# 512 weight columns moving instead of 256 in the output projection and the FFN's second product

## Chip, cores and metric

One core of a Trainium2 chip runs the kernel. The metric is the device time of one execution in microseconds (us).

## What is computed

Two layers of a hybrid diffusion backbone over 512 latent tokens and 256 context tokens of width 1024, in fp32. Each layer has four token mixers and a SwiGLU FFN. What matters here is how each of the two sublayers ends:

```python
def merge_branches(outs, gate_cols, w_brs, w_out):
    gates = jnp.split(jax.nn.sigmoid(gate_cols), N_BRANCH, axis=-1)
    mixed = sum(g * (o @ w) for g, o, w in zip(gates, outs, w_brs))
    return mixed @ w_out

def swiglu(h, w1, w3, w2):
    return (jax.nn.silu(h @ w1) * (h @ w3)) @ w2
```

`w_out` is 1024 x 1024, `w2` is 2816 x 1024. After each sublayer x += gate * RMSNorm(result), and the next one's input is the modulated RMSNorm of x. The last layer needs the latent tokens alone.

## The kernel before

The tokens are cut into blocks of 128: six in layer 0 (four latent, two context), four in layer 1. Every fp32 product is made of three fp32r matmuls: both operands are split into a high and a low part (`split`, line 544: a copy to fp32r, then the rest by a subtraction on VectorE), and high x high, high x low and low x high are added in PSUM. `wload` (line 566) brings a weight slice of 256 columns in chunks of up to four row blocks through the buffers `raw`, `wh` and `wl`, three of each (`wpool`).

*The two products.* `project_out` (line 1938) multiplies the transposed activations by 256 columns of the weight at a time (`qq`, four of them). For each token block `tb`, `gemm_tm` (line 596) runs the whole depth into one bank of PSUM: the block's tokens are the stationary side, the 256 weight columns move. One instruction on 128 x 256 then copies the result to `y` or adds it to `y`. The output projection is one such pass over the first 512 rows of `w_out` and one `project_last` (line 1959) over the other 512. The FFN's second product is cut by depth into parts of 6, 6, 6 and 4 row blocks. Ahead of each part come the first-product steps `up` for it (tile `ps_u`); the first three parts go through `project_out`, the last through `project_last`. That one loads all its weights first (three quarters of them into tiles `wr` of the general pool `pU`), then goes block by block, and ScalarE squares each result for the norm (`ssq`).

*The border.* After each pair of blocks `border_pair` (line 700) follows: the sum of the squares, `rstd` (line 552, 12 small VectorE steps), scale and gate, the addition to the residual `xres`, the store, and `norm_x` for the next sublayer. `pre_pair` (line 659) then transposes `y` on TensorE and applies scale and shift (`hf`). `finish_out` (line 2015) sets the blocks of the next pair between the border of a pair and its transposes. In the last sublayer each block has its own border, which stores the output.

*Buffers.* PSUM has eight banks: four single ones (`tA`, pool `psA`) and two tiles of two banks (`tS`, pool `psS`), which the attention scores use. Tiles of up to 128 x 512 come from `pW`, which has 19 of them (`y`, `gcast`, `xres`, `hf` and others); tiles of up to 128 x 256 come from seven small ones (`t1`).

*The order.* The program is written in a logical order and recorded by `Plan` (line 46). A list scheduler then gives every engine its own order, from costs of its own for each instruction (`cost`, line 141) and from free buffers: an instruction whose tile finds no free buffer is passed over, and later ones may go first. Matmuls to the same place in PSUM are kept together in groups of up to 12. The engines keep the order thus written. All instructions are issued at line 406, so every row of the trace has this line, and one goes by tile names. `fill("out")` and `fill("ffn")` put modulation work (`ps_mod`) into the same stages. `run` runs steps one after the other, `weave` spreads one list over another.

Of the kernel before, what the change touches and what calls it, by code (L numbers as in the profile page):

```python
# [12 lines left out]
F32 = mybir.dt.float32  # L13
# [395 lines left out]
def trace(plan: Plan, a: dict, out: bass.AP, dbg=None, depth=2):  # L409
# [174 lines left out]

    def gemm_fm(ps, w, c0, xT, nk):

        for s0, s1, p in ps:
            n = 0
            for k in range(nk):
                wh, wl = w(k)  # L590
                for wt, xt in ((wh, xT[0][k]), (wh, xT[1][k]), (wl, xT[0][k])):
                    PE.matmul(p[:, :s1 - s0], lhsT=wt[:, c0:c0 + 128], rhs=xt[:, s0:s1],
                              start=(n == 0), stop=(n == 3 * nk - 1))
                    n += 1
# [64 lines left out]
    def pre_pair(l, kind, p, yq, hT):  # L659

        col = 0 if p < 2 else 1
        t0 = p * 256
        for f in range(0, 8, 2):
            ps = tA("ps_tr")
            fv = tW("hf", (128, 2, 256))
            for i in range(2):
                for j in range(2):
                    PE.transpose(ps[:, i * 256 + j * 128:i * 256 + (j + 1) * 128],
                                 yq[f // 2][:, j, i * 128:(i + 1) * 128], ident)
            for i in range(2):  # L670
                ft = f + i
                scaled(fv[:, i], ps[:, i * 256:(i + 1) * 256], modc[l, "sc_" + kind][:, ft, col:col + 1],
                       modc[l, "sh_" + kind][:, ft, col:col + 1])
                split(hT[0][ft][:, t0:t0 + 256], hT[1][ft][:, t0:t0 + 256], fv[:, i])

    def norm_x(xs, yq):
# [9 lines left out]
        for i in range(2):  # L686
            for q in range(4):
                scaled(yq[q][:, i], xs[i][q // 2][:, (q % 2) * 256:(q % 2 + 1) * 256], r[:, i:i + 1])
# [11 lines left out]
    def border_pair(l, kind, p, yq, ssq, gcast, x_src, x_dst, nxt, part=(0, 1)):  # L700
# [6 lines left out]
        for i in part:  # L707
            for q in range(4):
                sl = slice((q % 2) * 256, (q % 2 + 1) * 256)
                V.scalar_tensor_tensor(yq[q][:, i], yq[q][:, i], r[:, i - part[0]:i - part[0] + 1], gcast[q // 2][:, sl], op0=ALU.mult, op1=ALU.mult)  # L710
                V.tensor_tensor(xs[i][q // 2][:, sl], xs[i][q // 2][:, sl], yq[q][:, i], op=ALU.add)
            for hf in range(2):
                SP.dma_start(x_dst(2 * p + i)[:, hf * 512:(hf + 1) * 512], xs[i][hf])
# [1105 lines left out]
    def first_pair(p):  # L1819
        cell = {}  # L1820

        def norm():
            xs = load_x(lambda tb: a["xin"][tb * 128:(tb + 1) * 128], p)
            cell["y"] = [tW("y", (128, 2, 256)) for _ in range(4)]
# [23 lines left out]
    for l in range(depth):  # L1848
# [89 lines left out]
        def project_out(w_src, xT, nk, first, y):  # L1938

            cell = {}  # L1940

            def one(qq, tb):
                def go():
                    if tb == 0:
                        cell["w"] = wload([w_src[:, qq * 256:(qq + 1) * 256]], nk)
                    ps = tA("ps_out")
                    gemm_tm(ps[:, :256], cell["w"], 256, xT, nk, tb)
                    if first and tb % 2 == 0:
                        y[tb // 2][qq] = tW("y", (128, 2, 256))
                    yq = y[tb // 2][qq][:, tb % 2]  # L1950
                    if first:
                        copy(yq, ps[:, :256])
                    else:
                        V.tensor_tensor(yq, yq, ps[:, :256], op=ALU.add)
                return go

            return [lambda qq=qq: run([one(qq, tb) for tb in tbs]) for qq in range(4)]

        def project_last(w_src, xT, y, ssq):
# [4 lines left out]
            def load(qq):  # L1964
                def go():
                    src = w_src[:, qq * 256:(qq + 1) * 256]
                    if qq == 3:
                        w[qq] = wload([src], 4)
                        return
                    raw = wpool.tile([128, 4, 256], F32, tag="raw", name="raw")  # L1970
                    SP.dma_start(raw, src.rearrange("(k p) c -> p k c", p=128))
                    parts = []
                    for i in range(2):
                        parts.append([tU("wr", (128, 2, 256), F32R) for _ in range(2)])
                        split(parts[i][0], parts[i][1], raw[:, 2 * i:2 * i + 2])
                    w[qq] = lambda k: (parts[k // 2][0][:, k % 2], parts[k // 2][1][:, k % 2])
                return go

            def one(tb):
                for qq in range(4):  # L1980
                    ps = tA("ps_out")
                    gemm_tm(ps[:, :256], w[qq], 256, xT, 4, tb)
                    yq = y[tb // 2][qq][:, tb % 2]
                    V.tensor_tensor(yq, yq, ps[:, :256], op=ALU.add)
                    S.activation(t1("junk"), yq, AF.Square, accum_out=ssq[tb // 2][:, tb % 2, qq:qq + 1])

            return [load(qq) for qq in range(4)], [lambda tb=tb: one(tb) for tb in tbs]

        def borders(kind, y, ssq, nxt, hT):
# [5 lines left out]
            def pair(p, part=(0, 1)):  # L1995
                def go():
# [6 lines left out]
                    border_pair(l, kind, p, y[p], ssq[p], gate[0],  # L2003
# [4 lines left out]
            def pre(p):  # L2008
                return lambda: pre_pair(nxt[0], nxt[1], p, y[p], hT)
# [17 lines left out]
        y = [[None] * 4 for _ in range(3)]  # L2027
        ssq = [sm.tile([128, 2, 4], F32, tag=f"ssq{p}", name="ssq") for p in range(3)]
# [6 lines left out]
        y = [[None] * 4 for _ in range(3)]  # L2035
        ssq = [sm.tile([128, 2, 4], F32, tag=f"ssq{p}", name="ssq") for p in range(3)]
# [143 lines left out]
```

## Time and profile before

| | us |
|---|---|
| time, median of 3 runs | 3187.0 (3186.23 to 3187.34) |
| the profiled execution | 3185.25 |
| its span | 3183.2 |
| TensorE busy in it | 3061.0 (96%) |
| weight loads busy | 2717.3 (85%) |
| VectorE busy | 2037.1 (64%) |
| ScalarE busy | 1303.6 (41%) |

The profile is one execution. PE is TensorE's matmuls, PEld its weight loads, which run beside them; DVE is VectorE, ACT ScalarE, SP the queue that issues the DMAs. An instruction is written as out<-in with its tiles' names. Matmuls are pipelined, so what one costs is the time from its start to the start of the next, and not its duration. The granted clock is a share of 2.4 GHz.

### The profile page before, as it was taken

What the parts mean: (1) busy time and instruction counts of PE and PEld (TensorE: products, weight loads), DVE (VectorE), ACT (ScalarE), POOL (GpSimd) and SP (SyncE); (2) the same over time, 40 slices, a digit from 0 to 9 for tenths busy, and PEclk for the clock granted to TensorE, in tenths of its full rate; (3) what the DMA queues carried; (4) which work ended last, traced back from release to release, by engine and by line L of the source; (5) the groups of instructions that cost most, each with busy time, mean ns of one, the idle gap of its engine ahead of it and who ended that gap; (6) DMA issues with size and microseconds to landing.
All of it is one profiled execution on the core that took longest, in us unless ns stands there. A gap on an engine that the chain in (4) does not pass through costs nothing.

```text
span 3183.2 us, 50019 instructions
## 1 busy us (share of the span) xinstructions
PE 3061.0 (96%) x19658; PEld 2717.3 (85%) x19658; DVE 2037.1 (64%) x4289; ACT 1303.6 (41%) x2633; POOL 10.2 (0%) x24
## 2 busy tenths in 40 slices
PE   7999999999999999999999999899999999999998
PEld 4888888898898779898998987788978879989997
DVE  8556769998677565622322379888968678653445
ACT  6432335455565343522111254335545565442222
POOL 0000000000000000000000000000000000000000
PEclk8999999899999999999999999999999999999999
DMA  8544422523223764423223245235345234243332
GB/s 291 160 134 131 142 84 78 173 62 121 70 87 111 247 196 123 120 70 103 62 71 105 88 133 189 78 110 157 86 136 157 89 95 153 74 123 100 93 93 80
DMA packets 297195, 380.02 MB, mean 119 GB/s; under 512 B 24813, under 2 KB 224830, under 8 KB 296960
## 3 DMA queue, kind: packets, MB, share of 16 engines
q1 hardware_dynamic: 294368, 369.75, 37.3%
q0 software_dynamic: 2592, 7.08, 0.8%
q8 instruction: 155, 2.54, 0.3%
q14 instruction: 80, 0.66, 0.1%
HBM read 318.94 MB, written 57.83 MB: 118 GB/s over the span
## 4 chain that ended last, share of the span: by engine, by line
PE 84%; DVE 10%; ACT 3%; issue 2%; DMA 1%; SPq 0%; DVEq 0%; ACTq 0%
PE ps_u L406 19%; PE ps_out L406 13%; PE ps_gate L406 12%; PE ps_proj L406 7%; PE ps_hyin L406 5%; PE ps_ssdin L406 4%; PE ps_mla L406 2%; PE ps_v L406 2%; PE ps_ms L406 2%; PE ps_qk L406 2%; PE ps_z L406 2%; PE ps_mod L406 1%; PE ps_pT L406 1%; PE ps_s L406 1%; PE ps_spec L406 1%
## 5 line engine op out<-in xcount | busy, mean ns | idle before, releaser
L406 DVE TENSOR_TENSOR wl<-raw,wh 128x1024 fp32r<-128x1024 f32 (+2 forms) x342 | 397.3, 1165 | 309.1 <-ACT wh L406 304.6
L406 PE MATMUL ps_u<-hf,wh 128*128 128x512 f32 (+1 forms) x2240 | 571.3, 345 | 6.8 <-DVE hf L406 2.6
L406 ACT CAST wh<-raw 128x1024 fp32r<-128x1024 f32 (+1 forms) x296 | 294.9, 997 | 425.9 <-PE ps_out L406 148.3
L406 PEld LDWEIGHTS ps_u<-hf,wh 128*128 128x128 f32 x2240 | 391.5, 190 | 58.2 <-DVE hf L406 3.1
L406 PE MATMUL ps_gate<-h,wh 128*128 128x512 f32 (+1 forms) x1568 | 417.8, 355 | 3.6 <-ACT wh L406 1.4
L406 PE MATMUL ps_u<-hf,wl 128*128 128x512 f32 (+1 forms) x1120 | 385.7, 344 | 0.0
L406 PEld LDWEIGHTS ps_gate<-h,wh 128*128 128x128 f32 x1568 | 274.3, 190 | 45.4 <-issue 2.0
L406 PE MATMUL ps_gate<-h,wl 128*128 128x512 f32 (+1 forms) x784 | 276.1, 352 | 0.4 <-DVE wl L406 0.4
L406 PEld LDWEIGHTS ps_u<-hf,wl 128*128 128x128 f32 x1120 | 213.1, 190 | 25.3
L406 PE MATMUL ps_out<-wh,gTh 128*128 128x256 f32 x760 | 217.1, 286 | 0.0
L406 PE MATMUL ps_out<-wl,gTh 128*128 128x256 f32 x760 | 215.1, 283 | 0.0
L406 PE MATMUL ps_out<-wh,gTl 128*128 128x256 f32 x760 | 215.0, 283 | 0.0
L406 PEld LDWEIGHTS ps_gate<-h,wl 128*128 128x128 f32 x784 | 149.0, 190 | 21.4 <-DVE wl L406 0.8
L406 PE MATMUL ps_hyin<-h,wh 128*128 128x512 f32 (+1 forms) x576 | 154.8, 357 | 2.0 <-DVE zb L406 1.7
L406 DVE TENSOR_TENSOR y<-y,ps_out 128x256 f32<-128x256 f32 x160 | 66.9, 420 | 140.2 <-PE ps_out L406 139.2
L406 PEld LDWEIGHTS ps_out<-wh,gTh 128*128 128x128 f32 x760 | 145.9, 192 | 6.8 <-issue 4.9
L406 PEld LDWEIGHTS ps_out<-wl,gTh 128*128 128x128 f32 x760 | 145.9, 192 | 0.1
L406 PEld LDWEIGHTS ps_out<-wh,gTl 128*128 128x128 f32 x760 | 145.8, 192 | 0.0
L406 DVE TENSOR_TENSOR s1t<-s1t,ps_u 128x512 f32<-128x512 f32 (+1 forms) x70 | 40.1, 572 | 140.8 <-PE ps_u L406 140.8
L406 PE MATMUL ps_ssdin<-h,wh 128*128 128x512 f32 (+1 forms) x480 | 120.8, 343 | 1.6 <-DVE acrow L406 1.0
L406 ACT ACTIVATE gate<-ps_gate 128x512 f32<-128x512 f32 (+1 forms) x98 | 50.8, 518 | 165.1 <-PE ps_gate L406 145.7
L406 PEld LDWEIGHTS ps_hyin<-h,wh 128*128 128x128 f32 x576 | 101.7, 190 | 17.9 <-issue 3.0
(462 smaller groups left out, 7067.5 us busy)
## 6 DMA issues: line engine op xcount, KB each, us to landing
raw<-in_w_in SPq DMA_DIRECT2D x120, 512.0 KB, 4.1
raw<-in_ffn_w SPq DMA_DIRECT2D x120, 512.0 KB, 3.9
w_mod<-in_mod_w SPq DMA_DIRECT2D x96, 512.0 KB, 4.6
raw<-in_w_in SPq DMA_DIRECT2D x52, 256.0 KB, 3.2
d_gt<-gate SPq DMA_DIRECT2D x32, 384.0 KB, 2.5
gate_in<-d_gt SPq DMA_DIRECT2D x32, 384.0 KB, 4.3
d_spec<-spec SPq DMA_DIRECT2D x40, 256.0 KB, 3.9
gsp<-d_spec SPq DMA_DIRECT2D x40, 256.0 KB, 3.7
```

The source lines that it names most:

```text
L406: getattr(engines[e], method)(*map(place, args), **{k: place(v) for k, v in kw.items()})
```

## The change

Both products now move 512 weight columns per matmul. `project_out` goes by halves `hf` of 512 columns. In a half, all token blocks hold an accumulator of one bank each at once: the first four lie side by side in the two double tiles `tS`, the two context blocks of layer 0 in single banks. The weights come by `wload2` in chunks of two row blocks by 512 columns, and each chunk is used for all blocks, six matmuls each, before the next. After the last chunk each accumulator is copied or added to `y`, 128 x 512 at a time. `project_last` still goes block by block with single banks, by halves. `y` is now a tile of 128 x 512 for each block and half (before: 128 x 2 x 256 for each pair and quarter), and the border's instructions are 512 wide. The squares' throw-away output `junk` moves from the small pool to `pW`. Pool sizes, the filled-in work and the scheduler stay as they are. This is the core of the diff; the removed bodies stand in the kernel above, and most of their lines are left out here:

```diff
+    def wload2(src):
+
+        parts = [wpool.tile([128, 2, 512], F32R, tag=t, name=t) for t in ("wh", "wl")]
+        raw = wpool.tile([128, 2, 512], F32, tag="raw", name="raw")
+        SP.dma_start(raw, src.rearrange("(k p) c -> p k c", p=128))
+        split(*parts, raw)
+        return parts
...
             for i in range(2):
                 for j in range(2):
                     PE.transpose(ps[:, i * 256 + j * 128:i * 256 + (j + 1) * 128],
-                                 yq[f // 2][:, j, i * 128:(i + 1) * 128], ident)
+                                 yq[j][f // 4][:, (f % 4 + i) * 128:(f % 4 + i + 1) * 128], ident)
...
-            for q in range(4):
-                scaled(yq[q][:, i], xs[i][q // 2][:, (q % 2) * 256:(q % 2 + 1) * 256], r[:, i:i + 1])
+            for hf in range(2):
+                scaled(yq[i][hf], xs[i][hf], r[:, i:i + 1])
...
-            for q in range(4):
-                sl = slice((q % 2) * 256, (q % 2 + 1) * 256)
-                V.scalar_tensor_tensor(yq[q][:, i], yq[q][:, i], r[:, i - part[0]:i - part[0] + 1], gcast[q // 2][:, sl], op0=ALU.mult, op1=ALU.mult)
-                V.tensor_tensor(xs[i][q // 2][:, sl], xs[i][q // 2][:, sl], yq[q][:, i], op=ALU.add)
             for hf in range(2):
+                V.scalar_tensor_tensor(yq[i][hf], yq[i][hf], r[:, i - part[0]:i - part[0] + 1], gcast[hf], op0=ALU.mult, op1=ALU.mult)
+                V.tensor_tensor(xs[i][hf], xs[i][hf], yq[i][hf], op=ALU.add)
...
         def project_out(w_src, xT, nk, first, y):
-            cell = {}
-            def one(qq, tb):
+            def half(hf):
                 def go():
-                    if tb == 0:
-                        cell["w"] = wload([w_src[:, qq * 256:(qq + 1) * 256]], nk)
+                    ps = []
+                    for tb in tbs[:4:2]:
+                        s = tS("ps_out")
+                        ps += [s[:, 0:512], s[:, 512:1024]]
+                    ps += [tA("ps_out") for _ in tbs[4:]]
+                    for k0 in range(0, nk, 2):
+                        w = wload2(w_src[k0 * 128:(k0 + 2) * 128, hf * 512:(hf + 1) * 512])
+                        for tb in tbs:
+                            sl = slice(tb * 128, (tb + 1) * 128)
+                            n = 0
+                            for k in range(2):
+                                for xp, wp in ((0, 0), (0, 1), (1, 0)):
+                                    PE.matmul(ps[tb], lhsT=xT[xp][k0 + k][:, sl], rhs=w[wp][:, k],
+                                              start=(k0 == 0 and n == 0), stop=(k0 == nk - 2 and n == 5))
+                                    n += 1
+                    for tb in tbs:
+                        if first:
+                            y[tb][hf] = tW("y")
+                            copy(y[tb][hf], ps[tb])
+                        else:
+                            V.tensor_tensor(y[tb][hf], y[tb][hf], ps[tb], op=ALU.add)
+                return go
+            return [half(hf) for hf in range(2)]
+        def project_last(w_src, xT, y, ssq):
+            w = {}
+            def load(hf, kp):
+                def go():
+                    src = w_src[kp * 256:(kp + 1) * 256, hf * 512:(hf + 1) * 512]
+                    if (hf, kp) == (1, 1):
+                        w[hf, kp] = [[p[:, k] for k in range(2)] for p in wload2(src)]
+                        return
+                    raw = wpool.tile([128, 2, 512], F32, tag="raw", name="raw")
+                    SP.dma_start(raw, src.rearrange("(k p) c -> p k c", p=128))
+                    w[hf, kp] = [[tU("wr", (128, 512), F32R) for _ in range(2)] for _ in range(2)]
+                    for k in range(2):
+                        split(w[hf, kp][0][k], w[hf, kp][1][k], raw[:, k])
+                return go
+            def one(tb):
+                sl = slice(tb * 128, (tb + 1) * 128)
+                for hf in range(2):
                     ps = tA("ps_out")
-                    gemm_tm(ps[:, :256], cell["w"], 256, xT, nk, tb)
...
+                    n = 0
+                    for k in range(4):
+                        for xp, wp in ((0, 0), (0, 1), (1, 0)):
+                            PE.matmul(ps, lhsT=xT[xp][k][:, sl], rhs=w[hf, k // 2][wp][k % 2], start=(n == 0), stop=(n == 11))
+                            n += 1
+                    yq = y[tb][hf]
+                    V.tensor_tensor(yq, yq, ps, op=ALU.add)
+                    S.activation(tW("junk"), yq, AF.Square, accum_out=ssq[tb // 2][:, tb % 2, hf:hf + 1])
+            return [load(hf, kp) for hf in range(2) for kp in range(2)], [lambda tb=tb: one(tb) for tb in tbs]
...
-        y = [[None] * 4 for _ in range(3)]
-        ssq = [sm.tile([128, 2, 4], F32, tag=f"ssq{p}", name="ssq") for p in range(3)]
+        y = [[None] * 2 for _ in tbs]
+        ssq = [sm.tile([128, 2, 2], F32, tag=f"ssq{p}", name="ssq") for p in range(3)]
```

## Rows read from the trace of the kernel before

**Rows 1.** The page: busy time by engine; the chain that ended last.

```profile
PE 3061.0 (96%) x19658; PEld 2717.3 (85%) x19658; DVE 2037.1 (64%) x4289; ACT 1303.6 (41%) x2633; POOL 10.2 (0%) x24
...
PE ps_u L406 19%; PE ps_out L406 13%; PE ps_gate L406 12%; PE ps_proj L406 7%; PE ps_hyin L406 5%; PE ps_ssdin L406 4%; PE ps_mla L406 2%; PE ps_v L406 2%; PE ps_ms L406 2%; PE ps_qk L406 2%; PE ps_z L406 2%; PE ps_mod L406 1%; PE ps_pT L406 1%; PE ps_s L406 1%; PE ps_spec L406 1%
```

**Rows 2.** Stretches by stage: length, busy time of engines (instructions), clock, DMA.

```profile
1277.70:1314.00 36.30, 30.02 (x233) 28.57 (x231) 31.00 (x115) 28.36 (x75) 0.00 (x0) 0.95 0.58 176
...
1560.50:1612.30 51.80, 51.80 (x434) 51.80 (x433) 18.26 (x34) 6.50 (x8) 0.00 (x0) 1.00 0.23 72
...
1837.20:1886.00 48.80, 40.94 (x309) 39.71 (x309) 35.01 (x122) 25.45 (x82) 0.00 (x0) 0.93 0.34 109
...
2787.70:2810.00 22.30, 14.78 (x96) 13.61 (x95) 19.77 (x77) 15.64 (x38) 0.00 (x0) 0.85 0.64 203
...
2969.00:3003.60 34.60, 34.60 (x289) 34.56 (x289) 14.65 (x25) 6.55 (x8) 0.00 (x0) 1.00 0.35 107
...
3171.10:3183.20 12.10, 0.22 (x2) 0.01 (x1) 8.26 (x34) 0.51 (x2) 0.00 (x0) 0.72 0.28 108
```

**Rows 3.** The same view, `ps_out` alone: both layers, two product stages.

```profile
1200.00:1900.00 700.00, 271.29 (x2160) 264.22 (x2160) 41.66 (x100) 16.39 (x44) 0.99 0.31 96
2700.00:3183.20 483.20, 173.72 (x1440) 173.41 (x1440) 27.75 (x66) 11.15 (x30) 0.99 0.31 94
...
1560.45:1612.30 51.85, 51.77 (x432) 51.85 (x432) 9.68 (x23) 0.00 (x0) 1.00 0.23 72
2869.21:2903.75 34.54, 34.54 (x288) 34.49 (x287) 0.00 (x0) 5.58 (x15) 1.00 0.35 106
```

**Rows 4.** The same view, `ps_u` alone: the FFN's first product.

```profile
2903.75:2969.05 65.30, 65.30 (x288) 53.89 (x288) 3.44 (x5) 3.59 (x6) 1.00 0.30 89
...
1612.30:1712.45 100.15, 100.08 (x576) 88.59 (x576) 6.22 (x11) 5.89 (x12) 1.00 0.21 61
```

**Rows 5.** The same view, `ps_proj` alone: a merge.

```profile
2719.65:2741.55 21.90, 21.88 (x96) 17.94 (x96) 4.80 (x7) 1.00 0.26 79
```

**Rows 6.** Timeline of PE at its start: start us, us, instruction.

```profile
2719.67 0.50 PE L406 MATMUL ps_proj<-oT_mh,wh 128*128 128x512 f32 x1 [0.92 <-DVE oT_ml L406]
2720.01 0.40 PE L406 MATMUL ps_proj<-oT_ml,wh 128*128 128x512 f32 x1
2720.25 0.40 PE L406 MATMUL ps_proj<-oT_mh,wl 128*128 128x512 f32 x1
```

**Rows 7.** Groups by shape, 1200 to 1900 us: busy us, mean ns, idle before.

```profile
L406 DVE TENSOR_TENSOR wl<-raw,wh 128x1024 fp32r<-128x1024 f32 x64 | 78.1, 1224 | 145.3 <-ACT wh L406 144.8
L406 ACT CAST wh<-raw 128x1024 fp32r<-128x1024 f32 x59 | 61.8, 1047 | 108.3 <-PE ps_u L406 58.1 <-PE ps_out L406 25.4 <-DMA raw<-in_ffn_w 19.9
L406 DVE TENSOR_TENSOR y<-y,ps_out 128x256 f32<-128x256 f32 x96 | 40.0, 420 | 84.8 <-PE ps_out L406 84.1
L406 DVE SCALAR_TENSOR_TENSOR y<-y,rs_y,gcast 128x256 f32<-128x256 f32 x46 | 20.2, 481 | 0.1
L406 ACT ACTIVATE junk<-y 128x256 f32<-128x256 f32 x48 | 19.8, 413 | 29.9 <-DVE rs_w L406 10.6 <-DVE y L406 10.5 <-DVE rs_y L406 5.8
...
L406 DVE TENSOR_TENSOR s1t<-s1t,ps_u 128x512 f32<-128x512 f32 x20 | 13.8, 688 | 63.0 <-PE ps_u L406 63.0
L406 ACT ACTIVATE junk<-xres 128x512 f32<-128x512 f32 x22 | 13.3, 603 | 10.6 <-DVE xres L406 8.1 <-ACT junk L406 2.3 <-ACT wh L406 0.2
```

**Rows 8.** DMA issues: count, KB each, median us to landing.

```profile
raw<-in_ffn_w SPq DMA_DIRECT2D x120, 512.0 KB, 3.9
...
xres<-in_xin SPq DMA_DIRECT2D x24, 256.0 KB, 3.6
```

**Rows 9.** PE's waits in two border stretches: us, times, longest.

```profile
PE ps_out L406 <- ACT hf L406: 3.4, 1, 3.4
...
PE ps_out L406 <- DVE s1t L406: 1.1, 1, 1.1
...
PE ps_tr L406 <- ACT y L406: 3.9, 2, 3.5
```

## The prediction and its working

> **What bounds the kernel now.** I read the page first, then the stretches by stage, then the two tiles that differ only in the width of what moves, and last the waits at the borders. TensorE is busy 3061.0 us, 96% of the span, VectorE 64%, ScalarE 41%, and of the chain that ended last the matmuls on `ps_u` hold 19%, those on `ps_out` 13% [rows 1]. By stage: in the products the PE's share is full (51.80 of 51.80 us, 34.60 of 34.60) at a granted clock of 1.00, the upper of the two levels, 2.4 GHz [rows 2]. The PE idles where one sublayer hands over to the next, 6.3, 7.9 and 7.5 us in stretches of 36.3, 48.8 and 22.3 us, with the clock at 0.95, 0.93 and 0.85; and for the last 12 us, when the output is normalised [rows 2]. So in the stages that the change rewrites nothing but PE time counts: what VectorE, ScalarE or the DMAs gain or lose there is hidden until it stops the PE.
>
> **Part 1, the width.** The trace holds 2160 `ps_out` matmuls in layer 0 and 1440 in layer 1 [rows 3], 256 columns moving in each. A stage of nothing else gives their pace: 432 in 51.85 us and 288 in 34.54 us, both 120.0 ns each [rows 3]. What 512 columns cost is in the FFN's first product: 288 of 512 columns in 65.30 us, 226.7 ns in layer 1; in layer 0 100.15 us hold 288 of each width, and with 288 x 120.0 = 34.6 taken off, 65.6 / 288 = 227.7 ns [rows 4]. Two narrow ones (240.0) become one wide one, so 13.3 ns are saved per pair in layer 1 and 12.3 in layer 0. The reason can be seen too: beside the narrow ones the weight load is busy 34.49 of 34.54 us, beside the wide ones 53.89 of 65.30 [rows 3, 4], and the change halves the loads with the matmuls. The sum: 1080 x 12.3 = 13.3 us and 720 x 13.3 = 9.6 us, together 22.9 us, all on the path. The wide pace could be worse here, since the weights move and the tokens stand still; the merge, another 512-wide product, ran 96 in 21.90 us, 228.1 ns with its first wait in it [rows 5], and at that pace the gain is 1800 x 11.9 = 21.4 us. Those are my ends, 21.4 and 22.9; I take 22.9 because the FFN's 512-wide matmuls have the same input type and a full stage around them.
>
> The Trainium skill, "TensorE: Matmul & The Clock Gate", section "Back-to-back issue gap", gives the spacing of one matmul as its columns at 2.4 GHz plus about 2.5 ns. By that, one wide for two narrow would save 2.5 ns only, an estimate of 4.5 us for 1800. The rows measure 11 to 14 ns above the column time at both widths, so here the trace disagrees with it; it stands among the rivals.
>
> **Part 2, the order inside a product.** Before, each block of 128 tokens ran its whole depth in one bank; now 4 (layer 1) or 6 (layer 0) accumulators stay open, and the PE changes bank after 6 matmuls, 1.4 us. In the 432-matmul stage there are 24 chains, so 24 changes of bank, and its mean is still 120.0 [rows 3]: a change costs nothing that shows. Coming back to an open bank is in no row. I take 0; at the upper end, 220 changes (1320 wide matmuls by 6) could each cost one wait like the first matmul of the merge, which started 0.34 us before its successor in place of 0.23 [rows 6], so 0.11 x 220 = 24 us. A gain is excluded by the pace already being the steady one.
>
> **Part 3, drains and the banks they hold.** One drain adds 512 columns in 0.688 us where two took 0.420 each [rows 7]: 160 adds (96 in layer 0, two thirds as many in layer 1) become 80, 67 us of VectorE become 55, beside PE's work. A 2-bank tile comes free only when both its blocks are drained. Inside the last round of a half, block 0 is done while blocks 1 to 3 still run, so the drains overlap the matmuls: after block 1, the PE has blocks 2 and 3 left, 2 x 6 x 0.227 = 2.7 us in layer 1. A drain with one weight subtraction ahead of it in VectorE's order takes 1.224 + 0.688 = 1.9 us [rows 7]. So there is 0.8 us of cover; with two subtractions ahead, 3.1 us, it is short by 0.4. This can happen at the half-to-half change, 4 in layer 1; in layer 0 the cover is 5.4 us and two blocks use the single banks. I take 0, with 4 x 0.4 = 1.6 us as the near end. What waits behind a late drain is the first group of the second half, and on VectorE the next weight subtraction.
>
> **Part 4, weights.** A chunk is now two row blocks by 512 columns: 512 KB, landing in 3.9 us, cast in 1.05 and subtracted in 1.22 [rows 7, 8]; it feeds 4 x 6 x 0.227 = 5.4 us of PE in layer 1, 8.2 in layer 0. Only one chunk is in use at a time, where the six-deep product used two for all its blocks, so two of the three buffers are free to run ahead: 10.9 us of cover for 6.2 us of supply. Each FFN part takes 6 loads in place of 8; on SP's queue 24 loads of 256 KB and their casts go and 12 of 512 KB come. Nothing, as long as the run-ahead holds.
>
> **Part 5, the borders and the end.** Per pair of blocks 8 scale-and-gate and 8 adds of 256 columns (8 x 0.481 + 8 x 0.420 = 7.2 us, the adds priced as those to y) become 4 and 4; the 512-wide add is 0.688 and the gated form above it by the same 0.06, say 0.75: 5.8 us [rows 7]. Against that the last drain and square of a block are longer, 0.688 - 0.420 and 0.603 - 0.413, 0.5 us. So about 1 us less for each of eight pairs, while the PE's cover between borders shrinks from 96 x 0.120 = 11.5 to 48 x 0.227 = 10.9 us. Only the pair that the PE waits for counts. In two of the borders the longest waits were 3.4 and 3.5 us, for a normalised or a transposed tile [rows 9]. I take 1 us of gain for the whole; a bound above is all the idle time of the three borders, 21.7 us, of which half could go at best since the statistics chain itself keeps its 13 small steps; a bound below stands under the third rival. The last 12 us keep their length: two add-and-gate pairs are shorter by 0.4, the last drain longer by 0.5.
>
> **The sum.** The profiled execution took 3185.25 us, its span 3183.2, 2.05 us lying around it; the median of three is 3187.0, 1.75 above the profiled one. 3185.25 - 22.9 - 1 = 3161.4, plus 1.75 is 3163 us.
>
> **Rivals.**
> *The hand-over costs something.* The order of every engine is written ahead from the planner's own costs, so a drain or a cast can stand behind a later wait. At the eight half-to-half changes and the borders, 1.2 us each on about eight places takes 10 us back: 3173. For it: the sums of part 3 leave 0.8 us only. Against it: in the product stages of before the PE never stopped, with drains as dense and two weight buffers tied up [rows 2].
> *The borders open up.* Shorter chains and earlier starts (the first rounds need two depth blocks only, where the last product of layer 0 now waits 1.1 us for `s1t` [rows 9]) could take half of the 21.7 us: 3163 - 11 = 3152.
> *Slower: the 19 wide buffers run out.* The squares' junk moves from the small pool into the wide one. In layer 0's borders 12 y, 2 gate rows, 4 residual tiles and 1 transposed tile make 19 already. If a square must wait there until the next pair's residual tiles or y come free, the statistics come late, then the transposes. Priced by one residual load, 3.6 us [rows 8], in eight pairs, 29 us, plus 3 for the clock, which stood at 0.85 where the PE waited most [rows 2]: 3163 + 32 = 3195. It is slower than before from 24 us on, 3 us for every pair; at two thirds of the price it is 3184, no change. Against it: a junk tile lives for 0.6 us, and a y tile comes free soon after.
> *It does not do what it says: a wide matmul takes as long as two narrow ones.* The merge's second wide matmul started 0.24 us before the third, exactly 2 x 0.120 [rows 6]. At 238 to 240 ns throughout the gain is 0 to 3.6 us: 3184, no change. Against it: in the same merge the mean of 96 is 228.1, in the FFN 226.7. By the Trainium skill's spacing rule of part 1 the time would be 3182, an estimate and in effect this same case.
> *Bank cycling drops the clock.* If each change of bank left the PE idle briefly, as at the upper end of part 2, the granted clock could fall: the new products are 1800 x 0.227 = 409 us, and at 0.93, as in one border [rows 2], they take 31 us more: 3194. The Trainium skill, same page, section "A second HAM failure mode: psum-queue depth-cycling", tells of a 512-column kernel that cycled its banks and lost throughput so. Here the 24 changes at clock 1.00 speak against it [rows 2, 3].
>
> **Chances.** Forecast, 3156 to 3169: 0.62. Hand-over: 0.12. Borders open: 0.11. Wide buffers: 0.06 at the full price, 0.03 at two thirds of it. Wide as slow as two narrow: 0.04. Bank cycling: 0.02. The measurement can tell about 0.2%, 6.4 us. Faster by more than that: 0.62 + 0.12 + 0.11 = 0.85. Within it: 0.04 + 0.03 = 0.07. Slower: 0.06 + 0.02 = 0.08. The range takes in the first three cases with the paces' ends, 3151 to 3177.
>
> **What would show it.** `ps_out` 1800 times, a pure product stage of layer 1 in 144 x 0.227 = 32.7 us where it was 34.5, of layer 0 in 49.2 where it was 51.8, clock 1.00. Drains 80 of 0.69 us. The three border stretches within 2 us of before. Wrong would be: a start-to-start of 512-wide `ps_out` well above 228, idle time before `ps_out` put down to y or to `wh` inside a product, or ScalarE's squares waiting for a buffer. A stretch outside these stages that grows or shrinks by more than 3 us would be the planner's reordering, which no row here can price; a few us of it lie within the range.

## The result, and the profile after

| | before | after |
|---|---|---|
| time, median, us | 3187.17 (3186.23 to 3187.91, 4 runs) | 3154.08 (3153.45 to 3155.08, 4 runs) |
| profiled execution, its span, us | 3185.25, 3183.2 | 3153.45, 3151.4 |

The ratio is 0.9897, with a 95% interval of 0.9879 to 0.9914: faster by 33.1 us. The forecast was 3163, with a range of 3151 to 3177: the direction and the range held, and the gain was 9 us larger than forecast.

The page of after: the busy time of each engine; from its last part, the FFN's weight loads.

```profile
PE 3029.3 (96%) x17858; PEld 2614.4 (83%) x17858; DVE 2001.8 (64%) x4074; ACT 1295.2 (41%) x2500; POOL 10.1 (0%) x24
...
raw<-in_ffn_w SPq DMA_DIRECT2D x132, 512.0 KB, 3.8
```

Beside [rows 1] the PE has 1800 matmuls fewer and is busy for 31.7 us less, which is the whole gain of the span (31.8): its idle time over the whole span is the same, 122.2 and 122.1 us. Part 1's sum for the width is 22.9 us, so some 9 us of PE time went from matmuls that the change leaves alone; the mean granted clock of the profiled execution is 0.981 before and 0.983 after. VectorE was busy for 35 us less and ScalarE for 8, beside the PE; part 5 below comes to where VectorE's time counts.

The stretches of after with `ps_out` alone, to be read beside [rows 3]: window, length, busy time of PE, weight loads, DVE and ACT (instructions), clock, DMA share, GB/s. First each layer, then one pure product stage of each.

```profile
1200.00:1900.00 700.00, 251.50 (x1080) 201.01 (x1080) 32.74 (x49) 12.98 (x23) 0.99 0.33 101
...
1555.90:1604.90 49.00, 49.00 (x216) 40.37 (x216) 7.21 (x11) 0.00 (x0) 1.00 0.25 75
2844.50:2877.15 32.65, 32.60 (x144) 26.87 (x144) 0.00 (x0) 3.23 (x6) 1.00 0.37 110
```

216 in 49.00 us are 226.9 ns each, 144 in 32.65 are 226.7 ns, at clock 1.00 and with the PE busy throughout. The weight load no longer fills the stage (26.87 of 32.65).

The stages of after, beside [rows 2]; all five engines now have a column. In order: layer 0's mixer border, the hand-over to layer 1 in two pieces, layer 1's mixer border, the last 12 us.

```profile
1275.20:1311.40 36.20, 30.09 (x193) 27.31 (x191) 30.74 (x107) 27.79 (x65) 0.00 (x0) 0.91 0.58 196
1826.70:1865.80 39.10, 35.50 (x163) 28.69 (x161) 30.02 (x87) 20.15 (x53) 0.00 (x0) 1.00 0.37 119
1865.80:1965.10 99.30, 96.19 (x540) 81.63 (x541) 95.52 (x231) 56.74 (x108) 2.11 (x4) 0.98 0.68 213
2762.65:2785.20 22.55, 14.28 (x94) 13.01 (x94) 18.79 (x68) 15.98 (x36) 0.00 (x0) 0.85 0.51 172
3139.40:3151.40 12.00, 0.15 (x1) 0.00 (x0) 8.19 (x27) 0.72 (x2) 0.00 (x0) 0.72 0.26 101
```

Two borders and the end are as long as before (36.20, 22.55 and 12.00, where they were 36.30, 22.30 and 12.10). The hand-over is not: 39.10 us where [rows 2] has 48.80, at clock 1.00 where it had 0.93. And the piece behind it, layer 1's first input products, is shorter as well; the same view of before, and the two pieces taken as one, before and after:

```profile
1886.00:1989.60 103.60, 98.18 (x541) 83.17 (x540) 96.97 (x241) 55.73 (x105) 2.11 (x4) 0.97 0.61 196
```

```profile
1837.20:1989.60 152.40, 139.12 (x847) 122.88 (x847) 131.98 (x363) 81.18 (x187) 2.11 (x4) 0.96 0.52 168
```

```profile
1826.70:1965.10 138.40, 131.69 (x703) 110.32 (x702) 125.55 (x317) 76.89 (x160) 2.11 (x4) 0.99 0.59 187
```

The piece behind holds the same 540 matmuls but for two, none of them touched by the change: 99.30 against 103.60 us.

To put the whole gain in its places, both traces are cut at the starts of the same eight matmuls. All table entries here and below are differences between such starts, in us, each from one execution (of the 23 of before on one chip the fastest took 3181.3 us and the slowest 3193.1, so a microsecond or two in one stretch shows little); "width" is what part 1's sum gives for the stretch.

| stretch | before | after less before | width |
|---|---|---|---|
| start to the last merge matmul of layer 0 (not touched) | 1210.9 | +0.9 | 0 |
| to layer 0's last mixer-border transpose (output projection) | 102.4 | -3.4 | -3.5 |
| to layer 0's last `ps_u` (FFN, three products) | 523.8 | -8.0 | -8.0 |
| hand-over: to the middle of layer 1's `ps_hyin` | 152.4 | -14.0 | -1.8 |
| to the last merge matmul of layer 1 (not touched) | 751.8 | +2.0 | 0 |
| to layer 1's last mixer-border transpose | 68.3 | -2.2 | -2.6 |
| to layer 1's last `ps_u` | 337.1 | -5.8 | -5.7 |
| to the end | 36.4 | -1.3 | -1.3 |
| sum | 3183.2 | -31.8 | -22.9 |

Five stretches give what the width alone gives, within 0.4 us. All that goes beyond it, 12.2 us, lies in one place, the hand-over, and 2.9 are lost again in work that the change doesn't touch. The hand-over's PE was busy for 139.1 us of 152.4 before, and for 131.7 of 138.4 after: 7.4 less busy, of which 1.8 is width and 5.6 go with the higher clock (0.96 and 0.99), and 6.6 less idle.

### The profile page after: what moved, and what is told of

Same layout as the page of the kernel before. It is cut to its first block, busy times and chain, and to the rows that moved or that the text cites. A ratio compares the mean times of both kernels' runs of the same rounds, so it can differ in the third digit from the quotient of the medians.

```text
span 3151.4 us, 45961 instructions
## 1 busy us (share of the span) xinstructions
PE 3029.3 (96%) x17858; PEld 2614.4 (83%) x17858; DVE 2001.8 (64%) x4074; ACT 1295.2 (41%) x2500; POOL 10.1 (0%) x24
## 5 line engine op out<-in xcount | busy, mean ns | idle before, releaser
L406 ACT CAST wh<-raw 128x1024 fp32r<-128x1024 f32 (+3 forms) x297 | 306.6, 1033 | 454.4 <-PE ps_out L406 177.4
L406 PE MATMUL ps_out<-wh,gTh 128*128 128x512 f32 x380 | 149.2, 392 | 0.2
L406 PE MATMUL ps_out<-wl,gTh 128*128 128x512 f32 x380 | 148.1, 390 | 0.0
L406 PE MATMUL ps_out<-wh,gTl 128*128 128x512 f32 x380 | 148.1, 390 | 0.0
L406 PE MATMUL ps_qk<-h,wh 128*128 128x512 f32 (+1 forms) x448 | 114.7, 346 | 1.4 <-ACT rope_sw L406 0.9
L406 PE MATMUL ps_mla<-wh,h 128*128 128x256 f32 (+1 forms) x544 | 104.6, 285 | 1.7 <-DVE zb L406 1.3
L406 PE MATMUL ps_hyin<-h,wl 128*128 128x512 f32 (+1 forms) x288 | 102.3, 355 | 0.0
L406 ACT ACTIVATE s1t<-ps_u 128x512 f32<-128x512 f32 (+1 forms) x70 | 35.3, 504 | 152.0 <-PE ps_u L406 152.0
```

The source lines that it names most:

```text
L406: getattr(engines[e], method)(*map(place, args), **{k: place(v) for k, v in kw.items()})
```

## Experiments

Three theories stood on the 10 us beyond the width. A: they are VectorE's time at the borders, from instructions 512 wide. B: they are the scheduler's order, which any edit draws anew. C: they come from the layout of `y`, one tile for each block and half, which ties no block to its neighbour. First the two halves of the change were taken apart.

### The new order of work with narrow matmuls (narrow_new_order)

```diff
-                    for k0 in range(0, nk, 2):
-                        w = wload2(w_src[k0 * 128:(k0 + 2) * 128, hf * 512:(hf + 1) * 512])
+                    for k0 in range(0, nk, 4):
+                        m = min(4, nk - k0)
+                        w = wload([w_src[k0 * 128:(k0 + m) * 128, qq * 256:(qq + 1) * 256]], m)
...
-                                    PE.matmul(ps[tb], lhsT=xT[xp][k0 + k][:, sl], rhs=w[wp][:, k],
+                                    PE.matmul(ps[tb], lhsT=xT[xp][k0 + k][:, sl], rhs=w(k)[wp],
```

Accumulators side by side and held open as after, but 256 columns of each move; `project_last` does its halves as two chains of 256.

> The changed kernel with its new order but 256 columns moving again: in project_out the accumulators of all blocks stay open over chunks of four row blocks by 256 columns (drains 256 wide), project_last runs each half as two 256-wide chains; squares and border stay 512 wide. If the width is worth 22.9 us (1080 x 12.3 + 720 x 13.3 ns) and the order nothing: 3154 + 22.9 = 3177 us, product stages at 120.0 ns per matmul. If the order or the earlier start of the products made part of the gain, it stays well below, 3165 to 3170. If open accumulators cost something that the width hid, above 3185.

Measured: 3193.39 us, ratio 1.0019 (1.001 to 1.0029). Its pure product stage, `ps_out` alone, and a stretch far ahead of any changed work with the wait that it holds (us, times, longest):

```profile
2875.95:2910.50 34.55, 34.55 (x288) 34.50 (x287) 0.00 (x0) 4.53 (x14) 1.00 0.35 107
```

```profile
1120.00:1160.00 40.00, 29.47 (x216) 20.29 (x219) 14.33 (x33) 11.39 (x24) 0.00 (x0) 0.83 0.78 264
```

```profile
PE ps_mod L406 <- DMA w_mod<-in_mod_w: 8.6, 3, 7.8
```

In the product 288 take 34.55 us, 120.0 ns each as in [rows 3]: the order inside a product and the open banks give and cost nothing there. The two FFN stretches are 1.3 us shorter and 2.4 longer than before's, where after's are 8.0 and 5.8 shorter: nearly all of that is the width. The hand-over is 7.9 us shorter than before's although no matmul in it is wider; part 5 below comes back to this. The 16 us above the expected time are in other places: the stretch up to layer 0's last merge matmul, with the same instructions as before, grew by 15.3 us, part of it the PE's wait of 8.6 us for a modulation weight, with the clock at 0.83 around it. Nothing of the edit acts there but the scheduler. That was the first sign for B, and the time, 3193, is outside every forecast made for it but the last, "above 3185", whose cause it doesn't have.

### Borders and layout without the wide products (border_wide_only, border_narrow, layout_only)

border_wide_only is the kernel before with `y` as after and the border's instructions as after; matmuls, drains and squares keep 256 columns:

```diff
-                    yq = y[tb // 2][qq][:, tb % 2]
+                    yq = y[tb][qq // 2][:, qq % 2 * 256:qq % 2 * 256 + 256]
...
-            for q in range(4):
...
             for hf in range(2):
+                V.scalar_tensor_tensor(yq[i][hf], yq[i][hf], r[:, i - part[0]:i - part[0] + 1], gcast[hf], op0=ALU.mult, op1=ALU.mult)
+                V.tensor_tensor(xs[i][hf], xs[i][hf], yq[i][hf], op=ALU.add)
```

border_narrow is the kernel after with the border's three kinds of instructions cut to 256 columns:

```diff
+            for q in range(4):
+                hf, sl = q // 2, slice((q % 2) * 256, (q % 2 + 1) * 256)
+                V.scalar_tensor_tensor(yq[i][hf][:, sl], yq[i][hf][:, sl], r[:, i - part[0]:i - part[0] + 1], gcast[hf][:, sl], op0=ALU.mult, op1=ALU.mult)
+                V.tensor_tensor(xs[i][hf][:, sl], xs[i][hf][:, sl], yq[i][hf][:, sl], op=ALU.add)
```

layout_only is border_wide_only with that same cut: every instruction as before, only the tiles of `y` are the new ones.

> The kernel before with the border alone made 512 wide (scale, gate, add, normalise; y kept per block and half); matmuls, drains and squares stay 256 wide. Theory A: the gain beyond the width, about 9 us, is VectorE time at the hand-over to layer 1, where VectorE was busy 77 of 82 us, so it comes back here: 3177 to 3182 us, and the stretch from the last FFN product of layer 0 to the first Hyena input product shrinks by 6 us or more. Theory B: those 9 us are the scheduler's order falling another way: a shift of either sign up to 8 us at places that have nothing to do with the border, 3179 to 3195, and no tie to that stretch.

> The changed kernel with its border alone cut back to 256-wide instructions (scale, gate, add, normalise). Theory A: the time beyond the width's is lost again, 3159 to 3164 us, at the hand-over to layer 1. Theory B: a shift of either sign, 3147 to 3162, wherever the order falls differently.

> The kernel before with y kept in one 128 x 512 tile per block and half in place of one 128 x 2 x 256 tile per pair and quarter; every instruction as before, 256 wide. Theory C, the layout itself (which y tiles come free when) makes the extra gain at the hand-over to layer 1: about 3178 us, that stretch 8 us or more shorter. Theory B, any new order of the scheduler moves that stretch: either sign, 3178 to 3195, and no reason for the same 8 us. Theory A, VectorE instruction width: no gain, 3187.

Measured: border_wide_only 3177.79, ratio 0.9973 (0.9961 to 0.9984); layout_only 3175.8, ratio 0.9972 (0.9963 to 0.9982); border_narrow 3153.84, ratio 0.9896 (0.9881 to 0.9911), the time of after. So in a freshly drawn order the width of the border's instructions adds nothing on either side, and the layout alone has the 8 us of border_wide_only. Where they lie, as the difference to before (border_wide_only's profiled execution was 5 us faster than its median):

| stretch | after | layout_only | border_wide_only | border_narrow |
|---|---|---|---|---|
| first, not touched | +0.9 | -3.9 | -0.9 | -0.7 |
| layer 0's FFN | -8.0 | 0.0 | 0.0 | -8.0 |
| hand-over | -14.0 | -5.9 | -8.0 | -11.0 |
| layer 1's FFN | -5.8 | 0.0 | 0.0 | -5.8 |

The hand-over of layout_only, one stretch for the two of before (48.80 in [rows 2] and the 103.60 above), and what its PE waited for:

```profile
1832.00:1978.50 146.50, 133.50 (x847) 117.11 (x846) 130.80 (x367) 82.24 (x189) 2.11 (x4) 1.00 0.54 176
```

```profile
PE ps_out L406 <- DVE y L406: 3.6, 2, 2.6
...
PE ps_out L406 <- ACT hf L406: 1.7, 1, 1.7
```

146.50 us where it was 152.4, and the difference is PE busy time: 133.5 us for the same matmuls that took 139.1 (847 records in both), at a clock of 1.00 in place of 0.96. The idle time is the same, 13.0 and 13.3 us; but the one wait of 3.4 us for `hf` [rows 9] is now 1.7, and the longest is 2.6. So 5.6 of the 5.9 us are not a wait that went: the idle time comes in shorter pieces, and the clock stays at its upper level. That the one makes the other isn't shown. Around one and the same wait, 2.6 us of `ps_out` for `y`, the clock was 0.89 in before and 1.00 in layout_only:

```profile
1855.00:1870.00 15.00, 12.42 (x92) 12.22 (x91) 12.33 (x49) 7.63 (x26) 0.00 (x0) 0.89 0.23 79
```

```profile
1849.80:1864.80 15.00, 12.43 (x104) 12.01 (x102) 13.12 (x53) 8.59 (x29) 0.00 (x0) 1.00 0.31 112
```

It isn't the chance of one execution either: in all ten of layout_only the mean clock of the span is 0.984 to 0.986, in the 17 of before beside them 0.979 to 0.983. Here the clock goes with the order; what in the order does it stays open.

### The last product narrow (last_narrow)

The kernel after with `project_last` of before (256 columns, squares in four parts):

```diff
-                for hf in range(2):
+                for qq in range(4):
...
+                    gemm_tm(ps[:, :256], w[qq], 256, xT, 4, tb)
+                    yq = y[tb][qq // 2][:, qq % 2 * 256:qq % 2 * 256 + 256]
+                    V.tensor_tensor(yq, yq, ps[:, :256], op=ALU.add)
```

> The changed kernel with project_last as it was before, 256 columns and 256-wide drains and squares, project_out wide. 480 of the 1800 wide matmuls (288 in layer 0, 192 in layer 1) are two narrow ones again: 288 x 12.3 + 192 x 13.3 ns = 6.1 us back, 3160 us if only the width counts. Theory A adds the drains and squares at the hand-overs, 1 to 3 us: 3161 to 3163. Theory B: 3152 to 3168.

Measured: 3165.1, ratio 0.9933 (0.9919 to 0.9948): 11.0 us above after, where the width of these 480 pairs is 6.1. `project_out`, which stays wide, keeps its pace to the last digit, and the hand-over has waits of the PE for banks that after doesn't have (the border's `norm_x` writes `junk` to a bank of `tA`):

```profile
2855.15:2887.80 32.65, 32.62 (x144) 26.84 (x143) 0.00 (x0) 3.23 (x6) 1.00 0.37 109
```

```profile
PE ps_out L406 <- ACT junk L406: 4.7, 3, 1.7
```

Against after, the hand-over is 5.8 us longer, 4.0 more than its width, layer 0's border 2.4 (1.8 of it width) and the first stretch, which isn't touched, 1.6. The excess is again at the hand-over, and again mixed with a new order; theory A's 3161 to 3163 is missed, B's 3152 to 3168 holds.

### The border's width with the order held (border_split_same_order)

To price A without B, the kernel after keeps the order of the scheduler, and every instruction on 512 columns that writes `y` or `xres` (drains, which read `ps_out`, and DMAs excepted) is issued as two of 256 at its place:

```diff
+                        names = [self.tiles[v.name][3] for v in args if isinstance(v, bass.AP) and v.name in self.tiles]
+                        wide = names[0] in ("y", "xres") and "ps_out" not in names and method != "dma_start" and self.cols(args[0]) == 512
+                        for sl in (slice(0, 256), slice(256, 512)) if wide else (None,):
+                            cut = lambda v: v[:, sl] if sl and isinstance(v, bass.AP) and self.cols(v) == 512 else v
```

> The changed kernel with the scheduler's order of every engine held exactly; only at issue each 512-wide border instruction (scale, gate, add, normalise) becomes two of 256 in its place. Theory A: VectorE time bounds the hand-overs, some 0.8 us per pair on eight pairs, so 3154 + 4 to 8 = 3158 to 3162. Theory B: the width of these instructions is worth next to nothing, 3153 to 3156, and border_narrow's equal time was no accident of order.

Measured: 3163.14, ratio 0.9944 (0.9928 to 0.9961), 9.1 us above after by the medians; the two ran on different chips, and by the ratios, each to before on its own chip, it is 15 us. Groups of after, 1200 to 1900 us (out<-in, shapes, count | busy us, mean ns | idle before, releaser):

```profile
L406 DVE SCALAR_TENSOR_TENSOR y<-y,rs_y,gcast 128x512 f32<-128x512 f32 x24 | 17.2, 746 | 0.1
L406 DVE TENSOR_TENSOR xres<-xres,y 128x512 f32<-128x512 f32 x24 | 15.8, 683 | 0.0
```

The same groups of border_split_same_order, whose instructions are issued at line 410, and its hand-over:

```profile
L410 DVE SCALAR_TENSOR_TENSOR y<-y,rs_y,gcast 128x256 f32<-128x256 f32 x48 | 20.3, 479 | 0.1
...
L410 DVE TENSOR_TENSOR xres<-xres,y 128x256 f32<-128x256 f32 x48 | 17.5, 417 | 0.0
```

```profile
1830.00:1971.50 141.50, 133.36 (x703) 111.38 (x701) 128.59 (x347) 78.50 (x167) 2.11 (x4) 0.98 0.56 184
```

Two narrow gates cost 0.958 us for 0.746, two narrow adds 0.834 for 0.683. The hand-over is 3.1 us longer than after's 138.4, half of it PE busy time at a lower clock (133.36 against 131.69); the front stretch is 2.9 longer, layer 1's border 1.2, the end 0.8. So A is real as long as the order is held: the two intervals don't meet, and VectorE's time is worth 8 us between the two traces, 9 to 15 by the times. border_narrow, with the same widths and an order made for them, lost none of it. Either the scheduler buys back what the instructions cost or its order happened to be a good one; in both cases A can't be read off a kernel whose order is drawn again.

### Three orders for each kernel (before, after and layout_only with the latency at 118 and 138 ns)

The scheduler takes 128 ns for the latency behind an instruction of VectorE and 135 behind ScalarE's. These two numbers change no instruction, only the order:

```diff
-        LAT = {"V": 128.0, "S": 135.0,
+        LAT = {"V": 138.0, "S": 145.0,
```

and 118 and 125 in the runs named v118.

> The kernel before, the same instructions, with the scheduler's assumed latency behind VectorE and ScalarE 10 ns longer (138 and 145 in place of 128 and 135), so that its order falls a little differently. Theory B: the time moves by several us, and the stretch of the hand-over to layer 1 by as much as in the variants (5 to 14 us) in some of these orders: 3175 to 3200. Theories A and C: within 3 us of 3187, the hand-over stretch unchanged.

> The kernel before with the scheduler's assumed latency behind VectorE and ScalarE 10 ns shorter (118 and 125). As for the longer one: by theory B 3175 to 3200 with the hand-over stretch moving, by theories A and C within 3 us of 3187.

> The changed kernel with the scheduler's assumed latency behind VectorE and ScalarE 10 ns longer (138 and 145). The kernel before came out 6 to 9 us slower in each of its two other orders. If the change is worth 22.9 us by width plus some 8 by the border's wide instructions in any order, this one is about 31 us under the kernel before in the same order: near 3162, between 3156 and 3168. If a part of the 33 us was a lucky order, the gap to the same order of before shrinks to 24 or less: 3168 or above. In all of them the pure product stages stay at 227 ns per matmul.

> The changed kernel with the assumed latencies 10 ns shorter (118 and 125). As for the longer ones: 3156 to 3168 if the gain does not hang on the order, 3168 or above if a part of it did.

> Layout only (y per block and half, all instructions 256 wide as before) in the order of the 10 ns longer latencies. If the layout itself gains 8 us it is 8 us under the kernel before in this order, about 3185; if its gain was one draw of the order it is anywhere from 3180 to 3200.

> Layout only in the order of the 10 ns shorter latencies. If the layout itself gains 8 us, about 3184; if its gain was one draw of the order, anywhere from 3180 to 3200.

| latency | before | layout_only | after | after less before |
|---|---|---|---|---|
| 128, as given | 3187.2 | 3175.8 | 3154.1 | -33 |
| 138 (v10) | 3193.3 | 3190.7 | 3180.3 | -13 |
| 118 (v118) | 3192.0 | 3186.9 | 3169.7 | -22 |

Each ratio is to the unperturbed kernel before on the same chip: before 1.0031 (1.0016 to 1.0046) and 1.003 (1.0015 to 1.0046), layout_only 1.0017 (1.0006 to 1.0029) and 0.9995 (0.9983 to 1.0007), after 0.998 (0.9969 to 0.9991) and 0.9949 (0.9929 to 0.9968). The last column by the ratios is -33, -16 and -26. Ten ns in an assumed latency move the kernel before by 5 to 9 us (8 and 9 beside the 3184.2 of the same chip) and the kernel after by 16 and 26.

Where it goes is shown by 2277 matmuls in the front of layer 0, which no edit touches: before as given, then before with 138, and the longest wait in the latter's window.

```profile
396.70:769.30 372.60, 352.38 (x2277) 323.17 (x2276) 320.56 (x662) 182.76 (x412) 0.00 (x0) 0.94 0.32 97
```

```profile
392.00:779.80 387.80, 358.68 (x2276) 326.50 (x2275) 321.18 (x655) 181.83 (x409) 0.00 (x0) 0.93 0.30 93
```

```profile
PE ps_off L406 <- DVE ssd_st L406: 5.5, 1, 5.5
```

387.8 us in place of 372.6, 9 us of it idle and 6 of it more busy time for the same matmuls. after_order_v10 has the same wait (5.2 us). The hand-over, as after less before of the same latency, is -14.0, -3.2 and -6.8 us, and the width's share of that is 1.8 each time (the profiled executions of before and layout_only with 118 and 138 were 3 to 7 us slower than their medians); layout_only less before is -5.9, +3.4 and -7.0. The FFN stretch of layer 1 gains its 5.8 us in all three.

What follows: the width's gain is in every order. So is a part of the hand-over's: the PE's idle time there falls by 6.6, 3.6 and 3.2 us in the three pairs. The rest goes either way. PE's busy time there, beyond the width, falls by 5.6 us, rises by 2.1 and falls by 1.9; and the mean clock of the profiled execution goes from 0.981 to 0.983 as given, but from 0.981 to 0.979 and from 0.983 to 0.981 in the other two pairs, and 0.002 of 3061 us of PE time are an estimated 6 us. The mean of the three differences is -23 us, by the ratios -25, and they spread over 20 us, so the mean is good to some 6. The width's sum is 22.9. About 10 of the 33 us therefore belong to the order that the scheduler happened to draw for this kernel. That is argued from three orders and not settled: it stays open whether the layout of `y` has a gain of its own, for layout_only is below before in all three (by 0.28%, 0.14% and 0.35%, the second within its noise), but at the hand-over in two of them only.

## Why the prediction was right, and where it was not

**Part 1, the width: right.** 226.9 and 226.7 ns where 227.7 and 226.7 were taken; the stages 49.00 and 32.65 us where 49.2 and 32.7 were forecast; stretch by stage the table above follows the sum. Narrow again, they take 120.0. The reason that it gave, a weight load that fills the narrow stage, isn't borne out: 256 columns more cost 226.7 - 120.0 = 106.7 ns, so 13.3 of the 120.0 ns don't depend on the width, and they are there with the load busy for all of the stage or for 82% of it. What the change saves is one such 13 ns with each matmul less; what the 13 ns are stays open. By the spacing rule of the Trainium skill, "TensorE: Matmul & The Clock Gate", "Back-to-back issue gap", the width would be worth an estimated 4.5 us; the section gives that rule for a matmul by itself, and says that in a stream of weight loads and matmuls both set the spacing. The rows, a weight load to each matmul, lie 11 ns above the rule at both widths, so the rule for one by itself doesn't hold here (the prediction's "11 to 14 ns above the column time" should read 13 to 14).

**Part 2, open banks: right.** The stages hold 36 and 24 changes of bank, return to open accumulators, and still run at the steady pace and at clock 1.00. With that the bank-cycling rival falls for these stages. The rival of the wide matmul as slow as two narrow ones falls by the same rows.

**Part 3, drains: right.** 80 adds, 0.685 us each, and no wait of the PE for a bank inside a product stage:

```profile
L406 DVE TENSOR_TENSOR y<-y,ps_out 128x512 f32<-128x512 f32 x48 | 32.0, 685 | 22.0 <-PE ps_out L406 21.6
...
L406 ACT ACTIVATE junk<-y 128x512 f32<-128x512 f32 x24 | 15.1, 628 | 20.6 <-DVE y L406 17.4 <-DVE rs_y L406 2.0 <-DVE ssx L406 0.9
```

These are layer 0's groups of after; the second also answers the rival of the 19 wide buffers: 17.4 of the squares' 20.6 us of waiting are put down to VectorE's `y`, their input, and no release of a wide buffer is named.

**Part 4, weights: right.** 132 loads of 512 KB in place of 120 [rows 8] and the smaller ones gone, and the product stages show no idle PE.

**Part 5, the borders: this is the term that was mis-sized.** It took 1 us for the whole; the hand-over gave 12.2 beyond the width. Three steps failed.

First, it set the PE's cover between two borders at 11.5 us before and 10.9 after, the matmuls of a whole pair, and left out the banks. The last product has the four single banks, which give the PE 4 x 12 x 0.120 = 5.8 us of work before VectorE must drain one, and 4 x 12 x 0.227 = 10.9 us after. In the hand-over of before the PE stands still for 2.58 us while VectorE works off a pair's gates and adds, and goes on during three drains that follow in one piece (VectorE's row covers all three):

```profile
1861.79 1.08 DVE L406 TENSOR_TENSOR y<-y,ps_out 128x256 f32<-128x256 f32 x3
...
1862.26 0.79 PE L406 MATMUL ps_out<-wr,gTh 128*128 128x256 f32 x2 [2.58 <-DVE y L406]
```

The PE's idle time before `ps_out` in the hand-over is 5.1 to 8.0 us in the eight traces in which the last product is drained 256 wide. Where it is drained 512 wide it is 1.1 to 2.0 us in five traces and 4.3 in the sixth, border_narrow. narrow_new_order, whose matmuls are narrow, is one of the five (1.5), so this goes with the banks and their drains and not with the matmuls' width. It is the part of the gain there that every order shows.

Second, it counted waits alone. 5.6 of the 12.2 us are the same matmuls at a higher clock; [rows 2] had the clock at 0.93 there, and the part left it out. In the other two orders it was -2.1 and 1.9, so most of it was luck of the order.

Third, it looked at the stretch of 48.8 us and not at the 103.6 behind it, where VectorE was busy for 96.97 us and the PE still lost 5.4; after, that piece gave another 4.3 us. With the order held, the border's wide instructions are worth 8 us or more, which is near eight pairs at the 1 us that the prediction worked out for each and then set aside; near in size only, since 2.9 of it lie in the front stretch. The waits of after in the hand-over, and in layer 1's border:

```profile
PE ps_gate L406 <- ACT junk L406: 2.6, 1, 2.6
PE ps_gate L406 <- ACT hf L406: 2.0, 1, 2.0
PE ps_out L406 <- DVE s1t L406: 1.1, 1, 1.1
```

```profile
PE ps_tr L406 <- ACT y L406: 6.1, 2, 4.5
```

The last product's waits for `hf` (3.4 us [rows 9]) and `y` (2.6) are gone; its matmuls read neither, so these were waits for a bank and not, as the prediction took the first, for a tile; the one for `s1t` is unchanged at 1.1. The 2.0 us for `hf` are another matmul's, of layer 1's first input product. In layer 1's border the wait for `y` grew from 3.9 to 6.1 us, its longest piece from 3.5 to 4.5, and the stretch is as long as before at the same clock of 0.85: there the shorter instructions gave nothing, so "shorter chains" is no rule for every border.

**The sum and the rivals.** 3163 was 9 us too high; the forecast's own range, 3156 to 3169, was missed by 2. The rival "the borders open up", 3152, came closest, and named the place; of its causes, an earlier start of the last product isn't in the rows, since the wait for `s1t` stayed.

**The scheduler's order: priced too low.** The prediction gave it "a few us". It measured 5 to 26 us for an edit that changes no instruction. By that, after in another order stands at 3170, inside the range of 3151 to 3177, or at 3180, outside it: that the time came out inside owes something to the order drawn. The direction was safe, since the width gains in every order; over the three orders the mean gain, 23 to 25 us, agrees with the prediction's own sum of 23.9, and the other 10 us are in no row of before.

## What to carry to other kernels

Where the PE is saturated, one 512-column matmul in place of two of 256 columns was worth 12 to 13 ns a pair; take both paces from stages that hold nothing else, and the sum holds to a few tenths of a us. Where a list scheduler writes the order, run both kernels in a few perturbed orders before crediting a cause with anything beyond that sum, and hold the order when one instruction's width is to be priced. At a border, price the work that the PSUM banks hold against what VectorE has in front of the next drain, and look at the stretch behind the wait as well: the same matmuls may run there at another clock.

## What was not expected of the hardware

The clock's share at the hand-over: the same matmuls (847 records) cost 139.1 us of PE time at a clock of 0.96 and 133.5 at 1.00, with the same idle time around them (13.3 and 13.0 us). The longest wait was 3.4 us in the one and 2.6 in the other, but around one wait of 2.6 us that both have, the clock was 0.89 in the one and 1.00 in the other. And VectorE's price for width: 512 columns in 0.685 us against 2 x 0.420 for the add, 0.746 against 2 x 0.479 for the gate, some 0.15 to 0.21 us saved with each instruction less.
